# A transformer block's first stage: the modulation products moved from VectorE to TensorE, 256 output channels at a time, and the first weight chunk's products of half the tokens with channels outermost

## The chip, the cores and the metric

The kernel runs as one program on one core of a Trainium2 chip. The metric is the device time of one execution in microseconds (us), taken as the median of three runs. The profile shows one execution, with the engines TensorE (PE; its weight loads are listed apart as PEld), VectorE (DVE), ScalarE (ACT), GpSimd (POOL) and the queue engine SyncE (SP), which only issues transfers here.

## The reference

One layer of a hybrid block: a modulation of the normalised input, one combined input projection, attention and a state-space branch side by side, their merge, and a feed-forward part. All inputs are float32; there are 1024 tokens of 1024 channels. Only the opening matters here:

```python
mod = jax.nn.silu(c) @ w_ada[l] + b_ada[l]          # c: 1024, w_ada: 1024 x 6144
shift1, scale1, gate1, shift2, scale2, gate2 = [m[:, None, :] for m in jnp.split(mod, 6, axis=-1)]
h = rms_norm(x, norm1_w[l]) * (1.0 + scale1) + shift1
proj = h @ w_in[l]
q, k, v, xBC, z, dt_raw, gates = jnp.split(proj, offsets, axis=-1)
```

So the first projection can start on a channel block of `h` as soon as 128 channels of `scale1` and `shift1` are there, and each of these 128 values is a sum over all 1024 rows of `w_ada`.

## The kernel before, in words

**The products.** Every large product is done in three passes of a reduced-precision float type: an operand is split into a high part and a low remainder (`hi`, `lo`), and TensorE adds hi·hi, hi·lo and lo·hi. The activation `h` is kept transposed, channels on the partitions, as `hhi[k][half]` and `hlo[k][half]` (printed as `hh` and `hl`): eight blocks `k` of 128 channels, two halves of 512 tokens. A weight chunk comes as `traw` (256 of the 1024 input channels, 400 output columns), and is split into `twh` on ACT and `twl` on POOL or DVE. Four such chunks make the first group of columns, `g=0`; `gemm_tm` multiplies it with eight token tiles `t`, 96 products (3 passes x 8 channel blocks x 4 token tiles) for each half of the tokens, into banks called `psq`.

**The first stage (lines 257 to 362).** Two of the six slices of `w_ada` are wanted first, 4 MB each. `mod_acc` loads a slice in eight row blocks of 128 x 1024 (`wada`, rows of 4 KB) and sums them on DVE, weighted by silu(c), into `macc` (line 219 once, line 221 seven times). `mod_col` then adds up the partitions with products against a column of ones (line 227: eight products, one moving column each) and DVE adds the bias. `scale_col` makes `s1`, the scale with the norm weight. In the meantime the first four token tiles `xs` are loaded, squared and summed on ACT (line 282), scaled (line 292), transposed on TensorE (line 298, `pst`) and copied to `xT`. When scale and shift of all 1024 channels are there, ACT writes `hh` (line 305), DVE the same in full precision (line 309) and DVE or POOL the remainder `hl` (line 154, the line of a helper). Then come the 96 products of the first half, then the 32 transposes of the second half's tokens, its `hh` and `hl`, and its 96 products.

**What sets the order.** SP and DVE keep the order in which this stage is written (`manual_schedule`); the other engines' order is set by a scheduler, and what the scheduler puts into SP's or DVE's row from later code can stand between. Each engine works its row off in order, so whoever stands behind a waiting instruction waits too.

Of the kernel before, what the change touches and what calls it, by code (L numbers as in the profile page):

```python
# [9 lines left out]
F32 = mybir.dt.float32  # L10
# [8 lines left out]
P = 128  # L19
# [71 lines left out]
def block(ctx: ExitStack, tc: tile.TileContext, ia, out, upto=99, dbg=None):  # L91
# [61 lines left out]
    def tt(e, o, a, b, op):  # L153
        e.tensor_tensor(out=o, in0=a, in1=b, op=op)  # L154
# [75 lines left out]
    def scale_col(dst, mi, n0):  # L230
        V.scalar_tensor_tensor(out=dst, in0=modc[:, mi], scalar=1.0, in1=vecT[:, n0:n0 + 8], op0=ALU.add, op1=ALU.mult)
# [24 lines left out]
    psq = psqs.enter_context(tc.tile_pool(name="psq", bufs=1, space=PSUM, side="right", reuse_waits="tile"))  # L256
    with tc.tile_pool(name="p0", bufs=1) as p0, tc.tile_pool(name="ps0", bufs=1, space=PSUM) as ps0:
        rows = p0.tile([120, P], F32, name="rows1")
        rows2 = p0.tile([104, P], F32, name="rows2")
        crow = p0.tile([8, P], F32, name="crow")  # L260
        dma(crow, ia["c"][0].rearrange("(t p) -> t p", p=P))
        ps = ps0.tile([P, 512], F32, name="psv", tag="psv", bufs=2)
        T.transpose(ps[:, :8], crow, ident[:8, :8])
        A.activation(sc, ps[:, :8], AF.Silu)

        def load_rows():
            for r0, nm in ((BA, "b_ada"), (N1, "norm1_w"), (CB0, "conv_b"), (N2, "norm2_w"), (SN, "ssd_norm_w")):
                src = ia[nm][0].rearrange("(t p) -> t p", p=P)
                dma(rows2[r0:r0 + src.shape[0], :], src)
            ps = ps0.tile([P, 512], F32, name="psv", tag="psv", bufs=2)  # L270
            T.transpose(ps[:, :104], rows2, ident[:104, :104])
            V.tensor_copy(vecT, ps[:, :104])

        xs, xT = {}, {}
        ss = p0.tile([P, 8], F32, name="ss")
        rs = p0.tile([P, 8], F32, name="rs")

        def x_load(t):
            xs[t] = p0.tile([P, D], F32, name="xs", tag="xs", bufs=4)
            dma(xs[t], x_in[t * P:(t + 1) * P, :])  # L280
            junk = p0.tile([P, D], BF16, name="junk", tag="junk", bufs=1)
            A.activation(junk, xs[t], AF.Square, accum_out=ss[:, t:t + 1])

        def x_unit(half):

            h4 = slice(half * 4, half * 4 + 4)
            rstd(p0, rs[:, h4], ss[:, h4], D, 4, G)
            for t in range(half * 4, half * 4 + 4):
                if half and t % 2:
# [4 lines left out]
        def x_turn(half, k):  # L294

            ps = ps0.tile([P, 512], F32, name="pst", tag="pst", bufs=2)
            for t in range(4):
                T.transpose(ps[:, t * P:(t + 1) * P], xs[half * 4 + t][:, k * P:(k + 1) * P], ident)
            return ps

        def x_mod(half, turned):
            for k in range(KT):
                src = turned(k)
                hi, lo = hhi[k][half], hlo[k][half]
                A.activation(hi, src, AF.Identity, scale=s1[:, k:k + 1], bias=modc[:, 0, k:k + 1])  # L305
                if k % 2 == 0:
                    fb = p0.tile([P, D], F32, name="xf", tag="macc", bufs=2)
                f = fb[:, (k % 2) * 512:(k % 2 + 1) * 512]
                V.tensor_scalar(out=f, in0=src, scalar1=s1[:, k:k + 1], scalar2=modc[:, 0, k:k + 1], op0=ALU.mult, op1=ALU.add)
                late.append((G if k % 4 in LOG else V, lo, f, hi.bitcast(F32), ALU.subtract))  # L310
                while len(late) > 1:
                    tt(*late.pop(0))
            tt(*late.pop(0))

        late = []

        def mod1(sl, between=None):
            g = mod_acc(p0, sl, bufs=7)
            n = 0
            try:  # L320
                while True:
                    next(g)
                    n += 1
                    if between:
                        between(n)
            except StopIteration as e:
                return e.value

        def mod2(acc, mi, sl):
            ps = ps0.tile([P, 512], F32, name="psv", tag="psv", bufs=2)  # L330
            mod_col(acc, sl, mi, ps)

        with tc.manual_schedule(engines={mybir.EngineType.SP, mybir.EngineType.DVE}):
            def first_half(n):
                if n <= 4:
                    x_load(n - 1)
                if n == 4:
                    x_unit(0)
                    for k in range(KT):
                        xT[k] = p0.tile([P, 512], F32, name="xT", tag="xT", bufs=8)  # L340
                        A.copy(xT[k], x_turn(0, k))
                if n == 6:
                    load_rows()

            scale = mod1(1, first_half)
            shift = mod1(0)
            mod2(scale, 1, 1)
            scale_col(s1, 1, N1)
            mod2(shift, 0, 0)
            loads = qkv_loads(0, G)  # L350
            first = [f() for f in loads[:2]]
            for t in range(4, 8):
                x_load(t)
            first += [f() for f in loads[2:]]
            x_mod(0, lambda k: xT[k])
            dma(masks[:, 1:5], ia["masks"][:, 1:5])
            dma(rows, ia["conv_w"][0].rearrange("k (t p) -> (k t) p", p=P))
            x_unit(1)
            x_mod(1, lambda k: x_turn(1, k))
# [4 lines left out]
        return dict(hhi=hhi, hlo=hlo, s1=s1)  # L364


    def gemm_tm(psp, tag, bufs, n, loads, evac, nxt_loads, first=None):

        w = first or [f() for f in loads]
        nxt = []  # L370
        for t in range(NT):
            if t >= 4 and nxt_loads:
                nxt.append(nxt_loads[t - 4]())
            half, sl = t // 4, slice((t % 4) * P, (t % 4 + 1) * P)
            ps = psp.tile([P, 512], F32, name=tag, tag=tag, bufs=bufs)
            o = ps[:, :n]
            for k in range(KT):
                hi, lo = w[k // 2]
                T.matmul(o, hhi[k][half][:, sl], hi[:, k % 2, :n], start=k == 0, stop=False)  # L379
                T.matmul(o, hhi[k][half][:, sl], lo[:, k % 2, :n], start=False, stop=False)  # L380
                T.matmul(o, hlo[k][half][:, sl], hi[:, k % 2, :n], start=False, stop=k == KT - 1)  # L381
                if k % 2:
                    yield 6 * n / 2400.0
            evac(t, o)
        return nxt
# [31 lines left out]
    with tc.tile_pool(name="p1", bufs=1, reuse_waits="tile") as p1, \  # L417
# [87 lines left out]
        for g in range(NKV):  # L505
            raws = {}

            def evac(t, ps):
                half = t // 4
                if t % 4 == 0:  # L510
                    raws[half] = p1.tile([P, 4, QKV_N], F32, name="qkvr", tag="qkvr", bufs=2)
                A.copy(raws[half][:, t % 4], ps)  # L512
# [4 lines left out]
            first = pump(gemm_tm(psq, "psq", 4, QKV_N, qkv_loads(g), evac,  # L517
                                 qkv_loads(g + 1) if g + 1 < NKV else z_loads(0), first))

        def dt_stream():  # L520

# [826 lines left out]
    with tc.tile_pool(name="p6", bufs=1, reuse_waits="tile") as p6:  # L1348
# [446 lines left out]
```

## Time and profile before

| | us |
|---|---|
| median of three runs (2547.34 to 2552.68) | 2547.74 |
| the profiled execution's own time | 2555.1 |
| its span | 2553.3 |
| TensorE busy / share of the span | 2422.2 / 95% |
| VectorE busy / share | 1779.8 / 70% |
| ScalarE busy / share | 1121.7 / 44% |
| GpSimd busy / share | 908.8 / 36% |
| TensorE busy in the first 37.0 us | 13.9 |
| start of the first half's products / of the second half's | 37.0 / 69.3 |

Over the span TensorE is the engine that is nearly always busy, so a microsecond of it saved or lost counts, if it isn't made good by a wait that gets shorter. The beginning is the exception: in the first 37 us it is idle for most of the time. The profiled execution is 7.4 us above the median of the runs.

### The profile page before, as it was taken

Reading aid. Unit: us, or ns where it says so; the run is one execution under the profiler, and the core shown is the slowest. Engines: PE = TensorE matmul, PEld = TensorE weight load, DVE = VectorE, ACT = ScalarE, POOL = GpSimd, SP = SyncE. Lnnn points to the kernel's source line nnn. Section 1 sums busy time; section 2 is a strip of 40 time slices with the busy share of each in tenths; the row PEclk is TensorE's granted clock in tenths of the full one; section 3 lists DMA queues with packets and bytes.
Section 4 is the critical chain, followed back from the end, with each engine's and each line's share of the span. In section 5 each row is a group of like instructions: output and inputs, shape, how many; then the busy total and the mean of one; then the engine's idle time right before and its main releaser. Section 6 shows DMA issues by size and latency. Waiting matters only on the chain. (4 is left out here: it accounts for less than half of the span.)

```text
span 2553.3 us, 32339 instructions
## 1 busy us (share of the span) xinstructions
PE 2422.2 (95%) x11403; PEld 1935.0 (76%) x11403; DVE 1779.8 (70%) x2199; ACT 1121.7 (44%) x1944; POOL 908.8 (36%) x672
## 2 busy tenths in 40 slices
PE   5999999999989999999899999999898999999999
PEld 5898777777767777777667767777686888888887
DVE  5756346898866666666577787636659888667794
ACT  5455513444546666666333344343333222264430
POOL 2310107677711111110346665514107875113200
PEclk9899999999999999999999999999998999999999
DMA  7653751233541212111666675466424645464522
GB/s 262 181 164 124 231 182 62 78 96 92 165 141 58 87 54 88 55 54 50 201 194 206 190 218 164 146 197 207 152 79 140 201 151 171 177 207 132 161 84 89
DMA packets 282162, 363.38 MB, mean 142 GB/s; under 512 B 33673, under 2 KB 166513, under 8 KB 282001
## 3 DMA queue, kind: packets, MB, share of 16 engines
q1 hardware_dynamic: 209841, 285.22, 35.7%
q10 hardware_dynamic: 72160, 76.11, 8.9%
q8 instruction: 90, 1.47, 0.2%
q14 instruction: 71, 0.58, 0.1%
HBM read 248.18 MB, written 113.06 MB: 141 GB/s over the span
## 5 line engine op out<-in xcount | busy, mean ns | idle before, releaser
L891 DVE TENSOR_REDUCE nm<-pss 128x1 f32<-128x1024 f32 x128 | 156.7, 1225 | 135.1 <-PE pss L889 133.7
L380 PE MATMUL psq<-twl,hh 128*128 128x400 f32 (+1 forms) x512 | 193.1, 379 | 7.4 <-DVE twl L154 5.4
L379 PE MATMUL psq<-twh,hh 128*128 128x400 f32 (+1 forms) x512 | 192.4, 381 | 3.4 <-ACT hh L305 1.3
L381 PE MATMUL psq<-twh,hl 128*128 128x400 f32 (+1 forms) x512 | 191.7, 376 | 0.0
L893 ACT ACTIVATE pf<-pss,nm 128x1024 f32<-128x1024 f32 x128 | 142.8, 1116 | 102.1 <-PE pst L904 99.3
L154 DVE TENSOR_TENSOR pl<-pst,ph 128x512 fp32r<-128x512 f32 x256 | 167.9, 683 | 27.6 <-ACT ph L168 27.6
L904 PEld LDWEIGHTS pst<-masks,pf 128*128 128x128 f32 x1024 | 118.3, 140 | 70.1 <-issue 29.7
L168 ACT CAST ph<-pst 128x512 fp32r<-128x512 f32 x256 | 146.4, 585 | 54.2 <-PE pst L904 41.0
L904 PE MATMUL pst<-masks,pf 128*128 128x128 f32 x1024 | 157.0, 276 | 11.7 <-DVE pl L154 9.7
L713 DVE SCALAR_TENSOR_TENSOR cacc<-pad,cwT,cacc 128x1024 f32<-128x1024 f32 x96 | 163.2, 1730 | 0.4
L154 POOL TENSOR_TENSOR av<-av,rz 64x512 f32<-64x512 f32 x32 | 41.3, 1290 | 326.5 <-DMA rz<-rz 158.5
L1673 PE MATMUL p<-o,o 128*128 128x512 f32 x400 | 155.2, 389 | 0.6 <-DVE o L154 0.6
L1672 PE MATMUL p<-o,o 128*128 128x512 f32 x400 | 153.8, 390 | 1.7 <-DVE ac L154 1.4
L1674 PE MATMUL p<-o,o 128*128 128x512 f32 x400 | 153.8, 389 | 0.0
L168 ACT CAST wop<-ws 128x512 fp32r<-128x512 f32 x116 | 71.7, 621 | 103.6 <-PE pp L1332 67.5
L380 PEld LDWEIGHTS psq<-twl,hh 128*128 128x128 f32 x512 | 98.5, 192 | 19.6 <-DVE twl L154 6.5
L154 POOL TENSOR_TENSOR sl<-sl 128x512 f32<-128x512 f32 x32 | 49.6, 1553 | 178.5 <-DVE o L154 72.4
L379 PEld LDWEIGHTS psq<-twh,hh 128*128 128x128 f32 x512 | 97.8, 192 | 15.8 <-ACT qkvr L512 1.7
L381 PEld LDWEIGHTS psq<-twh,hl 128*128 128x128 f32 x512 | 97.8, 191 | 11.9 <-issue 0.9
L1106 ACT ACTIVATE e<-psd 128x512 f32<-128x512 f32 x128 | 70.8, 595 | 74.6 <-PE psd L1104 61.4
L168 ACT CAST o<-sl 128x512 fp32r<-128x512 f32 x92 | 56.9, 623 | 105.0 <-PE p L1674 88.4
L941 PE MATMUL pv<-pl,v 128*64 128x512 f32 x256 | 102.0, 419 | 0.0
(424 smaller groups left out, 7133.0 us busy)
## 6 DMA issues: line engine op xcount, KB each, us to landing
ar<-r SPq DMA_DIRECT2D x100, 256.0 KB
wada<-in_w_ada_dram SPq DMA_DIRECT2D x48, 512.0 KB
r<-in_w_mlp_dram SPq DMA_DIRECT2D x32, 512.0 KB
sl<-in_w_mlp_dram SPq DMA_DIRECT2D x64, 256.0 KB
r<-in_w_in_dram SPq DMA_DIRECT2D x26, 512.0 KB
r<-ro ACTq DMA_DIRECT2D x52, 256.0 KB
r<-as SPq DMA_DIRECT2D x48, 256.0 KB
xb<-cst ACTq DMA_DIRECT2D x20, 512.0 KB
```

The costliest lines, as they stand in the source:

```text
L154: e.tensor_tensor(out=o, in0=a, in1=b, op=op)
L168: (e_hi or A.copy)(hi, src)
L379: T.matmul(o, hhi[k][half][:, sl], hi[:, k % 2, :n], start=k == 0, stop=False)
L380: T.matmul(o, hhi[k][half][:, sl], lo[:, k % 2, :n], start=False, stop=False)
L381: T.matmul(o, hlo[k][half][:, sl], hi[:, k % 2, :n], start=False, stop=k == KT - 1)
L713: V.scalar_tensor_tensor(out=acc, in0=pad[:, k:k + S], scalar=cwT[:, 24 * k + i:24 * k + i + 1], in1=acc, op0=ALU.mult, op1=ALU.add)
L891: V.tensor_reduce(out=nm, in_=ps, axis=AX.X, op=ALU.max, negate=True)
L893: A.activation(pfs[u], ps, AF.Exp, bias=nm, accum_out=zall[:, u:u + 1])
L904: T.transpose(pt[:, k], pf[:, (hf * 4 + k) * P:(hf * 4 + k + 1) * P], ident)
L1672: T.matmul(ps, a[:, 0, sl], b[0], start=start, stop=False)
L1673: T.matmul(ps, a[:, 0, sl], b[1], start=False, stop=False)
L1674: T.matmul(ps, a[:, 1, sl], b[0], start=False, stop=stop)
```

## The change

The sums over `w_ada`'s rows leave DVE. `ada_load(kh)` loads, for 256 output channels, all 1024 rows of both slices: two transfers of 1 MB with rows of 1 KB, four times. `ada_mod(k)` forms the 128 values of scale and of shift for channel block `k` on TensorE: 2 x 8 products with a 128 x 128 block of `w_ada` as the stationary operand and one column of silu(c) as the moving one. DVE adds bias and norm weight per block. `x_mod(0, k)` follows for that block straight from the transposes' bank (the copy `xT` is gone), then `first_gemm(k - 1)`, the twelve products of the block before with four token tiles whose banks stay open over all eight blocks; `gemm_tm` is given these banks as `made` and skips their products. The loads of `x` all have their own buffers now; small vectors are loaded from ACT's queue into tiles of their own; the scale of the norm is worked out on DVE in place of POOL; in the first half DVE takes over all the remainders `hl`.

```diff
+        for r0, nm in ((BA, "b_ada"), (N1, "norm1_w"), (CB0, "conv_b"), (N2, "norm2_w"), (SN, "ssd_norm_w")):
+            src = ia[nm][0].rearrange("(t p) -> t p", p=P)
+            vr = p0.tile([src.shape[0], P], F32, name=f"rows_{nm}")
+            adma(vr, src)
...
-            xs[t] = p0.tile([P, D], F32, name="xs", tag="xs", bufs=4)
+            xs[t] = p0.tile([P, D], F32, name="xs", tag="xs", bufs=8)
...
-            rstd(p0, rs[:, h4], ss[:, h4], D, 4, G)
+            rstd(p0, rs[:, h4], ss[:, h4], D, 4)
...
+            hi, lo = hhi[k][half], hlo[k][half]
+            A.activation(hi, ps, AF.Identity, scale=s1[:, k:k + 1], bias=modc[:, 0, k:k + 1])
+            f = p0.tile([P, 512], F32, name="xf", tag="xf", bufs=4)
+            V.tensor_scalar(out=f, in0=ps, scalar1=s1[:, k:k + 1], scalar2=modc[:, 0, k:k + 1], op0=ALU.mult, op1=ALU.add)
+            late.append((G if half and k % 4 in LOG else V, lo, f, hi.bitcast(F32), ALU.subtract))
...
+        def ada_load(kh):
+            ada[kh] = p0.tile([P, 2, KT, 2 * P], F32, name="wada", tag="wada", bufs=2)
+            for j in range(2):
+                dma(ada[kh][:, j], w_ada[:, j * D + 2 * kh * P:j * D + 2 * (kh + 1) * P].rearrange("(r p) c -> p r c", p=P))
+
+        def ada_mod(k):
+            w = ada[k // 2]
+            ps = ps0.tile([P, 512], F32, name="psv", tag="psv", bufs=2)
+            for j in range(2):
+                for r in range(KT):
+                    T.matmul(ps[:, j:j + 1], w[:, j, r, (k % 2) * P:(k % 2 + 1) * P], sc[:, r:r + 1], start=r == 0, stop=r == KT - 1)
+            tt(V, modc[:, 0:2, k], ps[:, 0:2], vecT[:, BA + k:BA + k + 9:8], ALU.add)
+            V.scalar_tensor_tensor(out=s1[:, k:k + 1], in0=modc[:, 1, k:k + 1], scalar=1.0, in1=vecT[:, N1 + k:N1 + k + 1],
+                                   op0=ALU.add, op1=ALU.mult)
+
+        def first_gemm(k):
+            hi, lo = w0[k // 2]
+            for t in range(4):
+                o, sl = first_ps[t][:, :QKV_N], slice(t * P, (t + 1) * P)
+                T.matmul(o, hhi[k][0][:, sl], hi[:, k % 2, :QKV_N], start=k == 0, stop=False)
+                T.matmul(o, hhi[k][0][:, sl], lo[:, k % 2, :QKV_N], start=False, stop=False)
+                T.matmul(o, hlo[k][0][:, sl], hi[:, k % 2, :QKV_N], start=False, stop=k == KT - 1)
...
-            scale = mod1(1, first_half)
-            shift = mod1(0)
-            mod2(scale, 1, 1)
-            scale_col(s1, 1, N1)
-            mod2(shift, 0, 0)
...
+            for t in range(4):
+                x_load(t)
+            ada_load(0)
+            w0.append(loads[0]())
+            vectors()
+            x_unit(0)
+            w0.append(loads[1]())
+            ada_load(1)
             for k in range(KT):
+                if k == 2:
+                    for t in range(4, 8):
+                        x_load(t)
+                if k in (2, 4):
+                    w0.append(loads[k // 2 + 1]())
+                    ada_load(k // 2 + 1)
+                ada_mod(k)
+                x_mod(0, k)
+                if k:
+                    first_gemm(k - 1)
+                if k == KT - 2:
+                    x_unit(1)
             tt(*late.pop(0))
+            first_gemm(KT - 1)
...
-            for k in range(KT):
+            for k in range(KT if t >= len(made) else 0):
```

What the change does to the engines' rows stands at three places.

**TensorE at the start.** The row of before, from its first instruction to the first products of `g=0` (`macc` is DVE's sum, `psq` the product's bank):

```order
L263 MATMUL psv<-masks,crow 128x8
L271 MATMUL psv<-masks,rows_392 128x104
L298 MATMUL pst<-masks,xs 128x128 x8
L227 MATMUL psv<-ones,macc 128x1 x8
L298 MATMUL pst<-masks,xs 128x128 x24
L227 MATMUL psv<-ones,macc 128x1 x8
L379 MATMUL psq<-twh,hh_0_347 128x400
L380 MATMUL psq<-twl,hh_0_347 128x400
```

The row now, one turn of the loop later (`hh_0_349` is channel block 1, `hh_0_351` block 2; lines 331 to 333 are `first_gemm`, line 322 is `ada_mod`, of which all sixteen products of a block stand between the products of the block two before it):

```order
L331 MATMUL psq<-twh,hh_0_349 128x400
L332 MATMUL psq<-twl,hh_0_349 128x400
L322 MATMUL psv<-sc,wada 128x1 x11
L333 MATMUL psq<-twh,hl_0_365 128x400 x4
L322 MATMUL psv<-sc,wada 128x1 x5
L302 MATMUL pst<-masks,xs 128x128 x4
L331 MATMUL psq<-twh,hh_0_351 128x400
L332 MATMUL psq<-twl,hh_0_351 128x400
```

Instead of sixteen one-column products ahead of all others there are 128, of which 32 stand ahead of the first large product and 96 in runs between the large ones.

**ScalarE ahead of the third channel block.** Before, from the splits of the weight chunks on:

```order
L168 CAST twh<-traw 128x2x400 x2
L305 ACTIVATE hh_0_347<-xT,modc,s_331 128x512
L305 ACTIVATE hh_0_349<-xT,modc,s_331 128x512
L282 ACTIVATE junk,ss<-xs 128x1024
L305 ACTIVATE hh_0_351<-xT,modc,s_331 128x512
```

And now:

```order
L168 CAST twh<-traw 128x2x400 x2
L304 ACTIVATE hh_0_347<-pst,modc,s_331 128x512
L286 ACTIVATE junk,ss<-xs 128x1024 x2
L304 ACTIVATE hh_0_349<-pst,modc,s_331 128x512
L286 ACTIVATE junk,ss<-xs 128x1024 x2
L168 CAST twh<-traw 128x2x400 x2
L304 ACTIVATE hh_0_351<-pst,modc,s_331 128x512
```

The `hh` of block 2 now stands behind the squares of the second half's four token tiles and behind the splits of the third and the fourth weight chunk.

**SyncE's queue.** Before, the 16 row blocks of `w_ada` come first (the first four token tiles between them), then two weight chunks of four transfers each, then the second half of `x`. Now, from the second quarter of `w_ada` on:

```order
L315 DMA wada<-in_w_ada_dram 128x8x256 x2
L284 DMA xs<-in_x_dram 128x1024 x4
L244 DMA traw<-in_w_in_dram 128x2x256
L244 DMA traw<-in_w_in_dram 128x2x64 x2
L244 DMA traw<-in_w_in_dram 128x2x16
L315 DMA wada<-in_w_ada_dram 128x8x256 x2
L244 DMA traw<-in_w_in_dram 128x2x256
```

Ahead of these rows stand the first four token tiles, the first quarter of `w_ada` and two weight chunks. The fourth weight chunk (the last row) comes behind the third quarter of `w_ada`; the last quarter stands behind three chunks of the next group of columns.

More of the change, by code (lines that the diff above doesn't have):

```diff
@@ L264, in block, with vectors @@
         A.activation(sc, ps[:, :8], AF.Silu)
[L266 to L269, printed above, removed]
+        def vectors():
             ps = ps0.tile([P, 512], F32, name="psv", tag="psv", bufs=2)
-            T.transpose(ps[:, :104], rows2, ident[:104, :104])
+            for r0, vr in vrows:
+                n = vr.shape[0]
+                T.transpose(ps[:, r0:r0 + n], vr, ident[:n, :n])
             V.tensor_copy(vecT, ps[:, :104])
-        xs, xT = {}, {}
+        xs, ada, w0 = {}, {}, []
         ss = p0.tile([P, 8], F32, name="ss")
@@ L286, in x_unit @@
             h4 = slice(half * 4, half * 4 + 4)
-            rstd(p0, rs[:, h4], ss[:, h4], D, 4, G)
+            rstd(p0, rs[:, h4], ss[:, h4], D, 4)
             for t in range(half * 4, half * 4 + 4):
-                if half and t % 2:
+                if t % 2:
                     V.tensor_scalar(out=xs[t], in0=xs[t], scalar1=rs[:, t:t + 1], scalar2=None, op0=ALU.mult)
@@ L292, in x_unit, with x_mod @@
                     A.activation(xs[t], xs[t], AF.Copy, scale=rs[:, t:t + 1])
-        def x_turn(half, k):
+        def x_mod(half, k):
             ps = ps0.tile([P, 512], F32, name="pst", tag="pst", bufs=2)
@@ L298, in x_turn @@
                 T.transpose(ps[:, t * P:(t + 1) * P], xs[half * 4 + t][:, k * P:(k + 1) * P], ident)
-            return ps
-        def x_mod(half, turned):
-            for k in range(KT):
[L303 to L312, printed above, removed]
-            tt(*late.pop(0))
@@ L315, in block @@
[L315 to L338, printed above, removed]
-                    for k in range(KT):
[L340 to L343, printed above, removed]
-            scale = mod1(1, first_half)
-            shift = mod1(0)
-            mod2(scale, 1, 1)
-            scale_col(s1, 1, N1)
-            mod2(shift, 0, 0)
[L350 to L355, printed above, removed]
+            hi, lo = hhi[k][half], hlo[k][half]
@@ new lines, in x_mod @@
+            A.activation(hi, ps, AF.Identity, scale=s1[:, k:k + 1], bias=modc[:, 0, k:k + 1])
+            f = p0.tile([P, 512], F32, name="xf", tag="xf", bufs=4)
+            V.tensor_scalar(out=f, in0=ps, scalar1=s1[:, k:k + 1], scalar2=modc[:, 0, k:k + 1], op0=ALU.mult, op1=ALU.add)
+            late.append((G if half and k % 4 in LOG else V, lo, f, hi.bitcast(F32), ALU.subtract))
+            while len(late) > 1:
+                tt(*late.pop(0))
+        def ada_load(kh):
+            ada[kh] = p0.tile([P, 2, KT, 2 * P], F32, name="wada", tag="wada", bufs=2)
+            for j in range(2):
+                dma(ada[kh][:, j], w_ada[:, j * D + 2 * kh * P:j * D + 2 * (kh + 1) * P].rearrange("(r p) c -> p r c", p=P))
@@ new lines, in first_gemm @@
+        def first_gemm(k):
[5 more added lines that the diff above has]
+                T.matmul(o, hlo[k][0][:, sl], hi[:, k % 2, :QKV_N], start=False, stop=k == KT - 1)
+        late = []
+        first_ps = [psq.tile([P, 512], F32, name="psq", tag="psq", bufs=4) for t in range(4)]
@@ new lines, in block @@
+        with tc.manual_schedule(engines={mybir.EngineType.SP, mybir.EngineType.DVE}):
+            loads = qkv_loads(0, G)
+            for t in range(4):
[6 more added lines that the diff above has]
+            ada_load(1)
+            for k in range(KT):
+                if k == 2:
[10 more added lines that the diff above has]
+                    x_unit(1)
+            tt(*late.pop(0))
+            first_gemm(KT - 1)
@@ L356, in block @@
             dma(masks[:, 1:5], ia["masks"][:, 1:5])
             dma(rows, ia["conv_w"][0].rearrange("k (t p) -> (k t) p", p=P))
-            x_unit(1)
-            x_mod(1, lambda k: x_turn(1, k))
+            for k in range(KT):
+                x_mod(1, k)
+            tt(*late.pop(0))
+            first = w0
         ps = ps0.tile([P, 512], F32, name="psv", tag="psv", bufs=2)
@@ L364, in block, with gemm_tm @@
         return dict(hhi=hhi, hlo=hlo, s1=s1)
-    def gemm_tm(psp, tag, bufs, n, loads, evac, nxt_loads, first=None):
+    def gemm_tm(psp, tag, bufs, n, loads, evac, nxt_loads, first=None, made=()):
         w = first or [f() for f in loads]
@@ L374, in gemm_tm @@
             half, sl = t // 4, slice((t % 4) * P, (t % 4 + 1) * P)
-            ps = psp.tile([P, 512], F32, name=tag, tag=tag, bufs=bufs)
+            ps = made[t] if t < len(made) else psp.tile([P, 512], F32, name=tag, tag=tag, bufs=bufs)
             o = ps[:, :n]
-            for k in range(KT):
+            for k in range(KT if t >= len(made) else 0):
                 hi, lo = w[k // 2]
@@ L517, in block @@
             first = pump(gemm_tm(psq, "psq", 4, QKV_N, qkv_loads(g), evac,
-                                 qkv_loads(g + 1) if g + 1 < NKV else z_loads(0), first))
+                                 qkv_loads(g + 1) if g + 1 < NKV else z_loads(0), first, () if g else first_ps))
         def dt_stream():
```

3 lines of the change are left out of this document (2 added, 1 removed).

## The prediction

> **What bounds the kernel now.** I read the page first, then the first 100 us in order of time, then the stage in stretches, and last the granted clock in stretches of 3.41 us.
>
> ```profile
> PE 2422.2 (95%) x11403; PEld 1935.0 (76%) x11403; DVE 1779.8 (70%) x2199; ACT 1121.7 (44%) x1944; POOL 908.8 (36%) x672
> 0.00:37.00 37.00, 13.94 (x66) 0.99 0.93 335
> 37.00:58.50 21.50, 19.41 (x98) 0.93 0.55 154
> 58.50:69.20 10.70, 6.23 (x33) 0.75 0.62 217
> 37.03 0.70 PE L379 MATMUL psq<-twh,hh 128*128 128x400 f32 x1 [1.26 <-ACT hh L305]
> 69.32 0.70 PE L379 MATMUL psq<-twh,hh 128*128 128x400 f32 x1 [1.25 <-ACT qkvr L512]
> ```
>
> The first row is the page's. The next three are stretches of the first stage: length, TensorE's busy time and instructions, granted clock, the transfers' busy share, GB/s. TensorE carries the kernel (95%), but until 37 us it works 13.9 us, while the transfers are 93% busy: the stage waits for 8 MB of `w_ada`. Then the first half's 96 products take to 58.5, and the second half's transposes and remainders to 69.32, where the second half's products begin. Behind that point the two programs have nearly the same order on all engines, with TensorE busy nearly throughout, so I take what is gained or lost at this point as gained or lost at the end. The question is when TensorE gets there.
>
> **The prices.** Rows of the order of time: start, duration, engine, line, count.
>
> ```profile
> 24.22 3.54 PEld L227 LDWEIGHTS psv<-ones,macc 128*128 128x128 f32 x16
> 33.83 1.86 PEld L227 LDWEIGHTS psv<-ones,macc 128*128 128x128 f32 x16 [0.99 <-DVE macc L221]
> 258.57 1.86 PEld L227 LDWEIGHTS psm<-ones,macc 128*128 128x128 f32 x16
> 27.70 5.50 PE L298 MATMUL pst<-masks,xs 128*128 128x128 f32 x24
> 58.49 1.03 PE L298 MATMUL pst<-masks,xs 128*128 128x128 f32 x8
> 38.53 0.54 PE L379 MATMUL psq<-twh,hh 128*128 128x400 f32 x1
> 38.86 0.54 PE L380 MATMUL psq<-twl,hh 128*128 128x400 f32 x1
> 40.47 0.34 PE L381 MATMUL psq<-twh,hl 128*128 128x400 f32 x1
> 40.65 0.34 PE L379 MATMUL psq<-twh,hh 128*128 128x400 f32 x1
> ```
>
> A one-column product with a 128 x 128 float32 block shows as two passes (8 products, 16 rows); a pass costs its weight load, 1.86/16 = 0.116 us, or 3.54/16 = 0.22 us at half clock. A transpose takes 0.13 or 0.23 us, a 400-column product (start to start) 0.18 or 0.33 us. The new `ada_mod` is of the same shape as line 227: 128 products, 256 passes, 29.7 us at the full clock and 56.6 at half. Removed are 32 passes (3.54 + 1.86 = 5.4 us, in time that was idle anyway), sixteen sums on DVE and eight copies on ACT; these lay ahead of 37 us beside the transfers, and give nothing but the earlier start. The vector loads on ACT's queue (five small ones ahead of `sc`) and the rest of `x_unit` are over before the first quarter of `w_ada` lands; I take them at nothing, and at 1 to 2 us of a later start if they were not.
>
> **When TensorE can start.**
>
> ```profile
> 5.65 0.75 DVE L219 TENSOR_SCALAR macc<-wada,sc 128x1024 f32<-128x1024 f32 x1 [4.65 <-DMA wada<-in_w_ada_dram]
> 14.74 1.06 ACT L282 ACTIVATE junk<-xs 128x1024 bf16<-128x1024 f32 x1 [1.41 <-DMA xs<-in_x_dram]
> 1934.00:1939.00 5.00, 4.38 (x19) 1.00 1.05 359
> 40.00:44.00 4.00, 4.00 (x24) 1.00 1.09 273
> ```
>
> Between the first and the eighth 512 KB transfer lie 9.09 us, 1.30 us each. Now four tiles of `x` come first: 5.65 to 9.6. The two halves of the first quarter have rows of 1 KB; a stretch in which the MLP's weights come with such rows moved 359 GB/s, so 2.9 us for 1 MB: 12.5 and 15.4. That is 24.5 us ahead of today's first product. TensorE then has 64 passes and eight transposes ahead of the first large product (channel blocks 0 and 1): at half clock 64 x 0.22 + 8 x 0.23 = 15.9 us, so 28.4.
>
> **Which clock.** Stretches of 3.41 us, cut where the granted clock changes; the fourth number is the clock. It is shown as 1.00 up to the first recorded change at 36.3, but the durations above tell that up to about 33 it was half.
>
> ```profile
> 26.11:29.52 3.41, 3.41 (x18) 1.00 1.03 417
> 29.52:32.94 3.42, 3.42 (x17) 1.00 1.11 329
> 32.94:36.35 3.41, 2.20 (x18) 1.00 0.88 266
> 36.35:39.76 3.41, 2.73 (x8) 0.51 1.01 391
> 46.59:50.00 3.41, 1.67 (x10) 1.00 0.00 0
> 60.24:63.66 3.42, 1.57 (x10) 1.00 0.56 212
> 63.66:67.07 3.41, 2.63 (x13) 0.51 0.99 370
> ```
>
> The clock changes at the ends of such stretches, by what TensorE did in them. 2.73 us of large products lifted it, 2.63 us of transposes did not: about 78% of a stretch. 1.67 us of large products kept it, 1.57 us of transposes did not: about 48%. Two rows tell of one-column products. The first is full (1.6 us of line 227, the rest transposes), yet the transposes behind it still ran at 0.23; the second stretch, full of transposes alone, lifted the clock. And 32.94 to 36.35 held 2.20 us, far over 48%, nearly all of it line 227, and the clock fell. So one-column products count for little or nothing. The Trainium skill, "TensorE: Matmul & The Clock Gate", "What's actually happening", gives the same window of 3413 ns and just the two clocks. Its section "HAM oscillation — how this bites in real kernels" draws the rule that TensorE stays fast as long as it has no idle gap over 3.4 us; by that the change would keep the full clock and end up near +9 us (the first rival below), not +35. The trace does not agree as far as one-column products fill the time: the clock fell after a stretch without any idle gap over 1 us.
>
> Now the loop: per channel block 32 passes, 4 transposes, 12 products. At full clock 3.7 + 0.5 + 2.2 = 6.4 us, at half 7.1 + 0.9 + 4.0 = 12.0 us. What counts is (0.5 + 2.2)/6.4 = 42% or 4.9/12.0 = 41%: too little to keep the clock. It is lifted only when a stretch falls almost wholly into the transposes and eight products that stand together (0.9 + 2.7 = 3.6 us at half clock). 78% of a stretch is 2.66 us, so of its 3.41 us of possible places 3.6 + 3.41 - 2 x 2.66 = 1.7 us do, one in two; the next stretch then does 6.8 us of work in 3.4. So 12.0 - 1.7 = 10.3 us a block.
>
> **The sum.** 28.4, then six blocks with `ada_mod` in them, 61.8: 90.2. The last 24 products and eight transposes hold no one-column products, 9.8 us at half clock; the clock rises after one stretch, 6.6 us: 96.8. Then the remaining 24 transposes, paced by ACT and DVE through two banks: before, 32 took from 58.5 to 69.32, 1.35 us for four; six times that is 8.1: the second half's products start at 104.9, against 69.32, +35.6. Both times the clock is then low or about to fall, which I take as equal (it cost 2.3 us before, bounds -2.3 to +2.3). One wait behind this point gets shorter:
>
> ```profile
> 97.14 0.46 PE L380 MATMUL psq<-twl,hh 128*128 128x400 f32 x1 [3.64 <-DVE twl L154]
> ```
>
> TensorE waits there for a remainder of the second group; now 27 products of the second group stand ahead of it, not 23, so 4 x 0.18 = 0.7 us less. In all +34.9, say +35: 2590 us against the profiled execution's 2555.1. That lies 7.4 us above the median of the runs, so 2583 by the median.
>
> The queues, edit by edit.
>
> ```profile
> 34.02 0.86 ACT L168 CAST twh<-traw 128x800 fp32r<-128x800 f32 x1 [0.20 <-DMA traw<-in_w_in_dram]
> 36.17 1.52 ACT L305 ACTIVATE hh<-xT,modc,s 128x512 fp32r<-128x512 f32 x2
> 39.08 0.68 DVE L154 TENSOR_TENSOR hl<-xf,hh 128x512 fp32r<-128x512 f32 x1
> ```
>
> ACT's `hh` of block 2 now stands behind the split of the fourth weight chunk, whose transfer stands behind the third quarter of `w_ada`: from 15.4, two chunks (0.82 MB at the 273 GB/s of 40 to 44 us, in which two such chunks came; 3.0), 5.8, four tiles 5.2, a chunk 1.5, 5.8, a chunk 1.5 are 38.2, then 0.86 for the split and 0.76 for `hh`: 39.8. At half clock TensorE comes to that product at 28.4 + 2 x 12 = 52, so this wait costs nothing; at full clock it does (below). The last quarter of `w_ada` waits behind three chunks of the next group; these wait for splits of about 42, so it lands near 52, and is wanted at half clock near 80, at full clock near 56. The remainders moved from POOL to DVE (0.68 us each) and the norm's scale lie beside 12 us of TensorE per block. The second half's `x` has its own buffers and is scaled in block 6, which takes that wait (ahead of 58 us before) off the path; it is already in the 8.1.
>
> **The rivals.**
> - One-column products count as work and the clock stays full from its first lift. Ahead of the first large product stand 8.5 us of full-clock work, some 5 us of it at half: 12.5 + 11 = 23.5. Two turns of 6.4 later, at 36.3, TensorE waits for the `hh` of block 2 to 39.8; from there six times 2.2, four `ada_mod` (14.8) and six groups of transposes (3.1, two of them the second half's): 70.9, with 8.1 more 79.0, +9.7 - 0.7 = +9: 2557. For it speaks only that busy time as the profile counts it would be nearly 100%; against it the two rows above.
> - The same without that wait (the scheduler's order on ACT costs nothing because transfers are faster): 3.5 us less, +5.5: 2553.
> - The clock stays at half through the whole loop: 28.4 + 6 x 12.0 + 9.8 + 8.1 = 118.3, +48: 2596. It would take stretches that never fall into the 3.6 us; the place of these stretches against the program is not mine to know.
> - Faster: the weight loads of the one-column products hide beside the large products. From 39.8 only 13.2 + 3.1 and 128 passes would be left; with those at nothing the second half starts at 64.2, -5.1 - 0.7 = -5.8: 2542. The point from which it decides is 5.8 us over 128 passes, 0.045 us each. Against it: 0.116 us each where sixteen stand in a row, also at 258.57 between large products, and here they stand in runs of 10 to 22.
> - The change doesn't do what it says: excluded by the order of the rows, where the products have moved.
>
> **How the numbers follow.** Mixed clock 66%, full clock with the wait 15%, without it 5%, half throughout 8%, hidden loads 4%, others (a start later by microseconds, another wait) 2%. The likeliest gives 2583; its own range, by the place of the stretches and by whether a one-column product counts for nothing or for a third, is 2572 to 2594. The range reaches down to the full clock with its wait and up to the half clock: 2556 to 2596, which leaves out about 1 in 10. About 5 us (0.2%) is what a measurement of this kernel can tell from no change: faster 4%, same 5% (half of the full clock without a wait, and some of the others), slower 91%.
>
> **What would show it.** Right: in the stage's stretches TensorE is busy from about 12.5 us on, the granted clock is 0.5 in most stretches between 36 and 90 us, passes of line 322 take 0.22 us, the first large product starts near 28, the second half's first (line 387) near 105, and behind it all is as before, 35 us later. Wrong: passes of 0.116 us throughout with line 387 starting at 75 to 82 (one-column products count); a wait of TensorE for line 304 near 40 us would go with it; or a stretch of DVE or of transfers as releaser of line 322, which would mean that a queue I took at nothing holds it.

## The result and the profile after

| | before | after |
|---|---|---|
| median of the runs (4 each) | 2548.84 us (2547.34 to 2552.68) | 2581.27 us (2575.21 to 2583.35) |
| ratio, 95% interval | | 1.0121 [1.0100, 1.0142] |
| the profiled execution; its span | 2555.1; 2553.3 us | 2579.94; 2578.1 us |
| TensorE busy | 2422.2 us (95%) | 2474.8 us (96%) |
| second half's first product | 69.32 us | 103.94 us |

The change makes the kernel 32.4 us slower by the medians (25 to 36 by the interval). TensorE is the engine that carries the kernel, and it has more to do: the page's row after, and the groups of the first 125 us that belong to the new products.

```profile
PE 2474.8 (96%) x11631; PEld 1990.4 (77%) x11631; DVE 1768.8 (69%) x2212; ACT 1116.6 (43%) x1934; POOL 901.7 (35%) x658
```

```profile
L322 PE MATMUL psv<-sc,wada 128*128 128x1 f32 x256 | 47.5, 316 | 5.5 <-DMA wada<-in_w_ada_dram 5.5
L331 PE MATMUL psq<-twh,hh 128*128 128x400 f32 x32 | 17.4, 544 | 0.0
```

The 256 one-column passes keep TensorE busy for 47.5 us. At the full clock they would take 29.7 (256 x 0.116). The large products suffer too: 544 ns each, where a product at full clock shows 340. Now the same stage in order of time (start, duration, engine, line, count):

```profile
13.24 4.82 PE L322 MATMUL psv<-sc,wada 128*128 128x1 f32 x22 [5.55 <-DMA wada<-in_w_ada_dram]
...
19.12 8.53 PE L322 MATMUL psv<-sc,wada 128*128 128x1 f32 x40
...
28.26 0.68 PE L331 MATMUL psq<-twh,hh 128*128 128x400 f32 x1
...
31.08 2.38 PE L322 MATMUL psv<-sc,wada 128*128 128x1 f32 x20
...
36.80 0.68 PE L331 MATMUL psq<-twh,hh 128*128 128x400 f32 x1
...
39.62 4.69 PE L322 MATMUL psv<-sc,wada 128*128 128x1 f32 x22
...
48.74 0.68 PE L331 MATMUL psq<-twh,hh 128*128 128x400 f32 x1
...
57.28 0.68 PE L331 MATMUL psq<-twh,hh 128*128 128x400 f32 x1
...
60.09 3.83 PE L322 MATMUL psv<-sc,wada 128*128 128x1 f32 x18
...
68.85 0.68 PE L331 MATMUL psq<-twh,hh 128*128 128x400 f32 x1
...
77.39 0.68 PE L331 MATMUL psq<-twh,hh 128*128 128x400 f32 x1
...
88.96 0.68 PE L331 MATMUL psq<-twh,hh 128*128 128x400 f32 x1
...
96.15 1.04 PE L302 MATMUL pst<-masks,xs 128*128 128x128 f32 x8
...
103.94 0.70 PE L387 MATMUL psq<-twh,hh 128*128 128x400 f32 x1 [1.25 <-ACT qkvr L520]
```

The reader sees TensorE start at 13.24 and a pass take 8.53/40 = 0.21 us, and less in a few stretches, as at 31 (2.38/20 = 0.12). The loop's last passes end near 88; then come the last products, the second half's transposes, and at 103.94 the product that stood at 69.32 before. The stage in stretches of 4 us (length, TensorE's busy time and count, granted clock, share of the transfers, GB/s):

```profile
36.00:40.00 4.00, 4.00 (x16) 0.50 1.14 297
...
52.00:56.00 4.00, 4.00 (x32) 0.90 1.09 354
56.00:60.00 4.00, 4.00 (x16) 0.50 0.19 60
60.00:64.00 4.00, 4.00 (x20) 0.50 0.00 0
...
72.00:76.00 4.00, 4.00 (x32) 0.93 0.00 0
...
88.00:92.00 4.00, 4.00 (x16) 0.50 0.00 0
```

TensorE has no gap in any of these rows, and yet the clock is at half in most of them. From 60 us on no transfer runs either, so nothing but TensorE holds the stage.

### The profile page after: what moved, and what is told of

It is laid out like the page before. It is cut to its first block, busy times and chain, and to the rows that moved or that the text cites. A ratio compares the mean times of both kernels' runs of the same rounds, so it can differ in the third digit from the quotient of the medians.

```text
span 2578.1 us, 32744 instructions
## 1 busy us (share of the span) xinstructions
PE 2474.8 (96%) x11631; PEld 1990.4 (77%) x11631; DVE 1768.8 (69%) x2212; ACT 1116.6 (43%) x1934; POOL 901.7 (35%) x658
## 5 line engine op out<-in xcount | busy, mean ns | idle before, releaser
L387 PE MATMUL psq<-twh,hh 128*128 128x512 f32 (+1 forms) x480 | 179.7, 379 | 2.1 <-ACT qkvr L520 1.2
L388 PE MATMUL psq<-twl,hh 128*128 128x512 f32 (+1 forms) x480 | 180.1, 376 | 1.0 <-DVE twl L154 1.0
L389 PE MATMUL psq<-twh,hl 128*128 128x512 f32 (+1 forms) x480 | 180.4, 377 | 0.0
L387 PEld LDWEIGHTS psq<-twh,hh 128*128 128x128 f32 x480 | 90.9, 190 | 14.5 <-ACT twh L168 1.6
L388 PEld LDWEIGHTS psq<-twl,hh 128*128 128x128 f32 x480 | 91.1, 190 | 12.2 <-DVE twl L154 1.8
L389 PEld LDWEIGHTS psq<-twh,hl 128*128 128x128 f32 x480 | 91.1, 190 | 11.6 <-issue 0.9
```

## The experiments

The theory: a one-column product costs its weight load and counts for almost nothing in what the clock is granted by. So the loop runs mostly at half clock (24 of the 34 us at the second half's start) and holds 256 passes that were not there (10 us). Rivals: the passes cost only because they stand between the large products; the reordered products cost by themselves; the loads or another queue hold the loop. All ratios are to the kernel before, run beside the experiment; in brackets the 95% interval. The column "start" is the second half's first product in the profile.

| | what | start, us | ratio |
|---|---|---|---|
| E0 | before, again | 69.9 | one run, 2554.71 us |
| E1 | 64 columns | 79.8 | 1.0014 [1.0004, 1.0023] |
| E2 | one of eight row blocks | 68.9 | 0.9986 [0.9977, 0.9995] |
| E3 | sums on VectorE | 83.4 | 1.0045 [1.0030, 1.0060] |
| E4 | 16 columns | 103.0 | 1.0085 [1.0067, 1.0102] |
| E5 | first part alone | 98.0 | 1.0071 [1.0057, 1.0085] |
| E6 | second part alone | 71.7 | 1.0000 [0.9989, 1.0010] |
| E7 | shared sums | 82.9 | 1.0021 [1.0013, 1.0030] |
| E8 | E7, sums sooner | 74.6 | 0.9996 [0.9986, 1.0006] |
| E9 | after, again | 104.5 | 1.0117 [1.0098, 1.0136] |
| E10 | E8, blocks in pairs | 69.9 | 0.9987 [0.9977, 0.9996] |
| E11 | 32 columns | 81.5 | 1.0037 [1.0022, 1.0052] |

**E0, the kernel before, unchanged.** No edit.

> The kernel before, unchanged, for a second profile of it. Open is where 10 us went: in the two profiles shown, the changed kernel is 34.6 us late at the first product of the second half, 24.5 us late at 725 us and at the end, while the medians differ by 32.4. Theory A: the profile of before was of an execution that lost some 6 us between 100 and 725 us for reasons of its own. Then this profile's own time is near the median, 2548, and its attention stage (line 889) begins near 718, not at 724.4. Theory B: the changed program makes good 10 us there in every execution, since waits behind the first stage get shorter. Then line 889 begins at 724 again.

The first product of the attention's line 889 (897 after) starts at 722.4 us here, against 724.7 in the first profile of before and 749.2 after: between the 718 of theory A and the 724 of theory B. This execution's own time, 2554.71, is again above the median of the runs beside it (2553.06). So 2.3 us of what the first pair of profiles shows as made good behind the stage belong to the profiled execution of before itself; the larger part does not.

**E1, 64 moving columns.**

```
-  T.matmul(ps[:, j:j + 1], w[...], sc[:, r:r + 1], ...)
+  T.matmul(ps[:, j * 64:(j + 1) * 64], w[...], sc[:, r:r + 1].to_broadcast([P, 64]), ...)
-  tt(V, modc[:, 0:2, k], ps[:, 0:2], ...)
+  tt(V, modc[:, 0:2, k], ps[:, 0:128:64], ...)
```

> The changed kernel with 64 equal moving columns in place of one in each of the 128 modulation products; results and weight loads are the same. Theory (one-column products don't count for the clock): 64 columns fill more than half of a pass, so the stage's stretches hold well over 48% of counted work, the clock stays at 1.0 from its first lift on, a pass takes 0.12 us, ScalarE's hh of block 2 becomes a wait of some 3 to 6 us near 40 us, and the second half's first product starts near 79 instead of 104: about 2557 us. Rival (passes are dear by their number and the clock does not depend on the columns, only on weight loads or on idle time): the clock stays at 0.5 in most stretches, passes take 0.22 us or more, the start is at 104 or later: 2581 us or more.

The products are the same in number and place, each now writes 64 equal columns. A row of the order of time and one of the stretches:

```profile
37.01 3.46 PE L322 MATMUL psv<-sc,wada 128*128 128x64 f32 x30
```

```profile
60.00:64.00 4.00, 4.00 (x33) 1.00 0.01 4
```

A pass takes 3.46/30 = 0.115 us with 64 columns as with one at the full clock, and the stretch that was busy 4.00 us at clock 0.50 after is busy 4.00 us at clock 1.00 here. The second half starts at 79.8, 24 us sooner, and nine tenths of the loss are gone. So the clock is what costs, and it does not follow the busy time; whether it follows the columns moved or a least width of a product is for E4 and E11. The wait of TensorE for `hh` of block 2 did not come: the scheduler had put that `hh` ahead of the split of the fourth weight chunk, and it ran at 36.55.

**E2, one of the eight row blocks in each sum.** `for r in range(KT)` in `ada_mod` becomes one step, so this kernel leaves out seven eighths of each sum.

> The changed kernel with one of the eight row blocks in each modulation sum: 16 products in place of 128; seven eighths of the sum over the rows of the modulation matrix are left out. All transfers stay. Theory (the passes and the clock that they cost are the whole loss): the stage is then held by ScalarE's hh of block 2 near 41 and by the last quarter of the modulation matrix near 54 us, the second half starts at 66 to 69 as before the change, and the time is 2544 to 2549. Rival (the new order of the queues, ScalarE's splits and squares ahead of hh, costs as much by itself): the second half starts later than 75 and the time stays over 2556.

With 224 of the passes gone the start is at 68.9 and the time 0.9986: without the passes the loss is gone. It is also about as early as this order starts the second half: the loads run up to 48 us (332 GB/s on average from 12 on), then come, among others, these two rows of the order of time.

```profile
52.83 1.70 PE L332 MATMUL psq<-twh,hl 128*128 128x400 f32 x4 [3.66 <-DVE hl L154]
...
68.91 0.70 PE L386 MATMUL psq<-twh,hh 128*128 128x400 f32 x1 [1.25 <-ACT qkvr L519]
```

**E3, the sums on VectorE**, eight operations of 128 x 2 x 256 per quarter, and one product with ones for each column. The remainders still due are written ahead of each sum.

```
+  V.tensor_scalar(out=acc, in0=ada[kh][:, :, 0], scalar1=sc[:, 0:1], ...)
+  V.scalar_tensor_tensor(out=acc, in0=ada[kh][:, :, r], scalar=sc[:, r:r + 1], in1=acc, ...)   # r = 1 to 7
-  for r in range(KT): T.matmul(ps[:, j:j + 1], w[...], sc[:, r:r + 1], ...)
+  T.matmul(ps[:, j:j + 1], acc[...], ones[:, 0:1], start=True, stop=True)
```

> The changed kernel with the sums over rows back on VectorE, 256 channels of scale and shift at a time (eight operations of 512 elements for each quarter, in place), and 16 one-column products against ones. So only the second part of the change, channels outermost and loads by 256 channels, is done. Theory: the loss lies in the one-column products; VectorE needs some 10 us per quarter (5.3 of sums, 4 of what it does for two blocks), from 15.5 on, so the last block is there near 56, the second half starts at 64 to 68, and the time is 2541 to 2549, at or below that before. Rival (channels outermost costs by itself, by open banks or by its order): over 2556.

The start came later than expected, at 83.4. VectorE's rows, and GpSimd's of the same time:

```profile
16.48 8.47 DVE L327 SCALAR_TENSOR_TENSOR wada<-wada,sc 128x512 f32<-128x512 f32 x7
...
31.75 6.98 DVE L327 SCALAR_TENSOR_TENSOR wada<-wada,sc 128x512 f32<-128x512 f32 x7
...
46.82 5.47 DVE L327 SCALAR_TENSOR_TENSOR wada<-wada,sc 128x512 f32<-128x512 f32 x7
```

```profile
18.69 4.15 POOL L154 TENSOR_TENSOR twl<-traw,twh 128x800 fp32r<-128x800 f32 x2 [18.25 <-ACT twh L168]
34.69 1.92 POOL L154 TENSOR_TENSOR twl<-traw,twh 128x800 fp32r<-128x800 f32 x1 [11.85 <-ACT twh L168]
```

Each quarter's sums, `s`, `xf` and `hl` stand one behind the other on VectorE, and TensorE waits for them (8.2 us the first time). VectorE is the bound in its turn: better than the change, worse than before. The time, 2564.4, lies where the rival had it (over 2556), but not for the rival's reason: E6 below shows that channels outermost costs nothing by itself.

**E4 and E11, 16 and 32 columns**: E1's edit with 16 and 32 in place of 64.

> The changed kernel with 16 equal moving columns in each modulation product instead of one (E1 had 64): a smaller dose of the same thing. Theory A (the clock is granted by moving columns, not by busy time): 16 columns fill 16/128 of the time in which a pass occupies TensorE, so a block's counted share rises from about 0.42 to 0.42 + 0.58 x 0.12 = 0.49. That is at the edge of what kept the full clock in the stretches of before (0.48) and far from what lifted it (0.78), so most of the loop stays at half clock: the second half's first product at 90 to 104, the time 1.006 to 1.012 of before. Theory B (any product wider than one column counts as full work): full clock from about 31 as in E1, the second half at 80, the time 1.000 to 1.003 of before.

> The changed kernel with 32 equal moving columns in each modulation product: between E4 (16, which stayed at half clock) and E1 (64, full clock). By the rows, 400 columns take 0.18 us, so 32 take 0.014 of a pass's 0.116 us, 12%; E1's 64 take 25% and E4's 16 take 6%. Theory A (columns are counted, and about 48% of a stretch keeps the clock): counted shares at full clock 0.42 + 0.58 x 0.12 = 0.49 here, 0.56 for E1, 0.46 for E4; at the edge, so the clock falls now and then: the second half's first product at 80 to 98, the time 1.002 to 1.009. Theory B (a threshold on the product's width itself, between 16 and 64): all or nothing, either as E1 (80, 1.001) with the clock full throughout or as E4 (103, 1.0085).

One stretch of E4, three of E11:

```profile
72.00:76.00 4.00, 4.00 (x19) 0.50 0.00 0
```

```profile
60.00:64.00 4.00, 4.00 (x34) 1.00 0.01 4
64.00:68.00 4.00, 4.00 (x24) 0.68 0.00 0
68.00:72.00 4.00, 4.00 (x25) 0.89 0.00 0
```

With 16 columns the loop is mostly at half clock from 46 us on and the start is at 103.0; with 32 the clock holds to 64, falls for one stretch (0.68 and 0.89 over 4 us each are 3.4 us at half clock), and the start is at 81.5; with 64 it does not fall in the loop. So the effect grows with the dose. A column takes 0.18/400 us, so 16, 32 and 64 columns fill 6, 12 and 25% of a pass of 0.116 us, and a block's counted shares at full clock are 0.46, 0.49 and 0.56: below, at and above the 48% that the prediction read from the stretches of before. (The expectations of E1 and E4 took more for a column: over half of a pass for 64, an eighth for 16.) E11 fits theory A: neither all of E1 nor E4. The 48% itself rests on two stretches of before and on these doses, and is no closer known than that.

**E5, the first part alone.** `first_gemm` and `first_ps` are taken out, so the 96 products stand behind the loop in the old order.

> The first part of the change alone: the modulation matrix by 256 channels and its sums on TensorE, but the first weight chunk's products in the old order, token tile by token tile, behind the loop. Theory A (the loss is the 256 passes at half clock, whatever stands between them): 13.2 + 256 passes x 0.22 = 56 + 32 transposes x 0.23 = 7 gives about 76 with the loads of x and weights under it, less some 4 for the passes that still run at full clock; then the 96 large products, the first ones at half clock (0.33 each for 4 to 7 us), the others at 0.18: 20 more, and 8 for the transposes of the second half: its first product at 97 to 106, the time 1.008 to 1.014 of before, as the whole change. Theory B (the passes cost because they stand between the large products and break their clock): without the mixture the second half starts at 90 or sooner and the time is 1.006 or less.

```profile
66.08 6.83 PE L322 MATMUL psv<-sc,wada 128*128 128x1 f32 x32
...
77.71 0.34 PE L384 MATMUL psq<-twl,hh 128*128 128x400 f32 x1
```

The loss is there without the mixture, 1.0071, though a little less than expected (1.008 to 1.014). All passes take 6.83/32 = 0.213 us up to 73.7, but the large products, together now, lift the clock after 4 us and nearly all run at 0.18 us instead of 0.33.

**E6, the second part alone**, on the kernel before: `first_gemm(k - 1)` behind block k of `x_mod(0, ...)`.

> The second part of the change alone: the kernel before, modulation by whole rows on VectorE and GpSimd, but the first weight chunk's products of the first four token tiles with channels outermost, each block behind the next one's ScalarE and VectorE work. Theory A (this part is worth nothing by itself: before, TensorE waited only 2.1 us for a weight half and 1.3 us for an hh tile inside these products): the second half's first product at 67 to 71, the time 0.998 to 1.001 of before. Theory B (the reordering costs by itself, since the four sums are now all finished at the end and their evictions come in one bunch): the second half's first product at 72 or later, or the bunch's wait moved behind it, the time 1.002 or more.

```profile
PE psq L393 <- DVE twl L154: 4.2, 1, 4.2
```

By itself the order of the products changes nothing: 1.0000. The start is 1.8 us later than in E0, and the wait for a remainder behind it (4.2 us here, 2.7 and 3.6 in the two profiles of before) is still there.

**E9, the changed kernel again**, beside another set of runs of before.

> The changed kernel as it is, a second time, beside the same runs of the kernel before as E8. It is to tell how much of its loss the second part of the change (channels outermost) makes with the first, since E5 without it took 1.0071 [1.0057, 1.0085]. Theory A (mixing the large products into the passes makes them run at half clock: 44 of the 96 products or so at 0.33 instead of 0.18 us, 6 us): 1.010 to 1.013 again, the second half's first product at 101 to 106. Theory B (the 1.012 of the first measurement lay high by the chip or the runs): 1.006 to 1.009, as E5.

1.0117 again, as theory A had it: the second part, worth nothing alone, costs about 0.5% (1.0117 against 1.0071, the intervals apart) when the passes are there, since it puts the large products among them. In the profiles the start moves from 98.0 to 104.5, which is 6.5 us, while 0.46% are 12. Another 3 us of these are lost in the 185 us behind the start: E5 begins there at full clock (0.45 us for the first product), the changed kernel at half (0.70). The rest stays open.

**E7, E8 and E10, a version built from these.** 64 columns; rows 0 to 3 of each quarter summed on VectorE in place, 4 to 7 on TensorE, with a product by ones for VectorE's part; the second half's transposes inside the loop.

```
...
+  if k % 2 == 0: ada_sum(k // 2)          # E7; E8 and E10: quarters 2 and 3 behind x_mod(0, 3) and x_mod(0, 5)
   ada_mod(k)                              # E10: ada_mod(k) and ada_mod(k + 1) at even k
   x_mod(0, k)
   if k: first_gemm(k - 1)
-  if k == KT - 2: x_unit(1)
+  if k == 3: x_unit(1)
+  if k > 3: x_mod(1, 2 * (k - 4)); x_mod(1, 2 * (k - 4) + 1)
...
-  for k in range(KT): x_mod(1, k)         # behind the loop
```

> A candidate, built from what E1 to E3 showed: 64 columns (the clock stays full), four of the eight row blocks of each quarter summed on VectorE in place and the other four on TensorE with one product by ones for VectorE's part (160 passes instead of 256, 11 us less of TensorE), and the transposes of the second half inside the loop from the fourth channel block on instead of behind it. Theory A (TensorE is the bound of E1's loop, VectorE of E3's, so half each takes both below the loads, which end at 48): last quarter at 48, two blocks of 160/8 x 2 = 40 passes x 0.115 = 4.6, 24 products x 0.18 = 4.3 and 8 transposes = 1, some waits of 4: the second half's first product at 60 to 68, the time 0.994 to 0.999 of before. Theory B (VectorE's chain of sums, s, xf and hl in one queue is the bound as in E3, and the second half's transposes now wait in it too): second half at 72 to 82, the time 1.000 to 1.005.

```profile
45.93 0.43 PE L328 MATMUL psv<-ones,wada 128*128 128x64 f32 x2 [2.84 <-DVE wada L321]
...
66.04 0.69 PE L328 MATMUL psv<-ones,wada 128*128 128x64 f32 x2 [3.71 <-DVE wada L321]
```

The time, 1.0021, is in theory B's range, and the start, 82.9, just behind it (72 to 82): TensorE waits for sums that stand on VectorE behind work nobody waits for yet, and runs at half clock after each of the two waits.

> E7 with VectorE's sums of the third and fourth quarter put earlier in VectorE's queue: directly behind the xf of the first half's blocks 3 and 5, ahead of the second half's scaling and of the second half's xf, where E7 had them behind. Theory A (E7 lost 2.8 and 3.7 us of TensorE waiting for these sums, and with each wait a stretch at half clock, 44 to 56 and 64 to 76 us): without the waits the clock stays full; passes 160 x 0.116 = 18.6, 16 groups of transposes 8.5, 96 products 17.3, 4 more for the half clock at the start, from 13.2 on: 61.6, with some waits 62 to 70 for the second half's first product, the time 0.995 to 0.999 of before. Theory B (what stands behind TensorE's start is bound by the loads, which end at 48, and by ScalarE and VectorE in turn, so that waits only move): 74 to 82, the time 1.000 to 1.003.

The waits for these sums fell from 7.1 us to 1.4, and the time is that of before. Theory A had the start too early (62 to 70, here 74.6, in theory B's range); the time lies between the two. One row of VectorE shows what was left: the `s` of block 7 comes only here.

```profile
67.76 1.03 DVE L330 SCALAR_TENSOR_TENSOR s<-modc,vecT 128x1 f32<-128x1 f32 x1
```

> E8 with the modulation products of both channel blocks of a quarter together, ahead of the first of the two blocks' transposes and hh, so that the odd block's modulation does not stand on VectorE behind the second half's xf (in E8 block 7's sums were through TensorE at 61.4, but s for it came at 67.8). Theory A (the tail of E8 is this order on VectorE): block 7's hh 4 to 6 us sooner, the second half's first product at 67 to 72, the time 0.997 to 0.9995 of before. Theory B (the remaining distance is swallowed behind this point, as E6's and E1's late starts were, or the wait moves to hl): 72 to 76 or an unchanged time, 0.999 to 1.001.

```profile
69.91 0.45 PE L399 MATMUL psq<-twh,hh 128*128 128x400 f32 x1
```

The start is at 69.9, as before, and at the full clock (0.45, where before shows 0.70 after its wait). 0.9987 [0.9977, 0.9996] is some 3 us, as theory A had it. It is only just told from no gain, and this is the one version here with all its sums that comes out ahead of before.

## Why the prediction was right

The forecast was 2583 us, +35; measured 2581.27 and +32.4, and again 2582.36 and +30.5 in E9. The mechanism, passes at half clock in a loop that is lifted now and then, is what the runs show. Its terms by their own steps:

| term | forecast | measured |
|---|---|---|
| TensorE's start | 12.5 | 13.24 |
| 64 passes and 8 transposes at half clock | 15.9 | 15.0 (13.24 to 28.26) |
| six blocks at a mixed clock | 61.8 | 60.7 (28.26 to 88.96) |
| last 24 products and 8 transposes | 6.6 | 7.2 (88.96 to 96.15) |
| 24 transposes of the second half | 8.1 | 7.8 (96.15 to 103.94) |
| start of the second half | 104.9 | 103.94 |

The blocks show the mixed clock itself. Between the rows of line 331 at 28.26, 36.80, 48.74, 57.28, 68.85, 77.39 and 88.96 lie 8.54 us three times and 11.57 to 11.94 three times, where the prediction had 12.0 and, one time in two, 3.4 less; in E9's profile three blocks are again short and three long.

**The clock.** The step that decided, that one-column products count for little or nothing, is shown by E1, E11 and E4, in that order of dose. The rule of the Trainium skill weighed in the prediction ("TensorE: Matmul & The Clock Gate", "HAM oscillation — how this bites in real kernels": fast as long as there is no idle gap over 3.4 us) is not borne out: from 56 to 64 us TensorE was busy 8.00 of 8.00 us at clock 0.50. The first rival, full clock, is the kernel of E1. That its start, 79.8, lies near the 79.0 of that rival is luck: the first large product came at 28.68 and not at 23.5, and the wait for `hh` up to 39.8, which the 79.0 contains, did not come. Its price by the ratio is 3.6 us (1 to 6) and not 9.

**The queues** were rightly taken at nothing. `hh` of block 2 was ready at 41.85 + 0.77 = 42.6, wanted at 48.74; forecast 39.8 and 52.

```profile
41.85 0.77 ACT L304 ACTIVATE hh<-pst,modc,s 128x512 fp32r<-128x512 f32 x1
```

The last quarter was asked for only at 48.2, when TensorE's passes over the second quarter had ended and its buffer was free, a wait that the prediction's working does not have. It cost nothing: the transfers of the stage ended by 60, and the quarter was wanted at 71.66.

**The term that was mis-sized** is what lies behind the point: the prediction gave it -0.7, "TensorE waits there for a remainder", and took the rest as equal. Two stretches, E0's and after's first 30 us behind the second half's start:

```profile
69.90:100.00 30.10, 27.33 (x132) 0.90 0.54 157
```

```profile
103.90:134.00 30.10, 30.02 (x148) 0.90 0.57 163
```

In the same time TensorE gets through 148 instructions instead of 132, 16 x 0.18 = 2.9 us. The wait for `twl` is not 0.7 us shorter but gone (0.4 us of it are left in E9): VectorE had 34 us more for it. The clock in the two stretches, which the prediction took as equal, is equal: 0.90.

From the second half's start to line 570 (578 after) it is 187.9 us in E0 and 184.5 after (185.2 in E1); in E2, which starts as before does, it is 187.0, so the gain comes with the late start. Between there and the attention's product of line 889 another 4 to 5 us go (464.5 us in E0, 460.7 after, 459.5 in E9); TensorE's busy time over the same 1959 instructions falls by 2.8 and 5.5 us, so this is mostly clock (0.98 in E0, 0.99 after and in E9). Behind that product the distance stays: 26.8 us there and at line 1053 of before, 26.3 at line 1332, 25.2 at the end (after against E0).

To take what is lost at this point as lost at the end was therefore too much by 9 us in the profiled pair, and by 2 to 4 us by the medians, which lie 30 and 32 us apart. How much of the 4 to 5 us is chance of where the clock's stretches fall stays open; the same part takes 463.7 us in E1, 462.5 in E2 and 466.9 in E11, in no order of their starts. The two profiled executions, on which the working can be followed, lie 24.8 us apart (2579.94 against 2555.1), where it has 34.9: that the median comes within 2 us of the forecast is in part luck.

**The loss by parts**: +34.6 us at the second half's start. E1 leaves 10 of it at full clock, the bare passes; 24 are the clock. Of these 24, some 6 come from mixing the large products in (E5, 98.0 against 103.94).

## What to carry to other kernels

Read the granted clock and the columns together, not TensorE's busy time: a run of one-column products looks 100% busy and pulls its neighbours to half speed. If such products must stand among large ones, widen them with equal columns up to what their weight load hides (64 cost nothing here), or give half of the sum to another engine. Before moving sums from idle time under a transfer onto the engine that carries the kernel, count its passes at both clocks.

## What was not expected of the hardware

Widening a float32 product from one to 64 columns cost no time (0.115 us a pass, 0.116 with one). VectorE's 128 x 512 sums took 5.47/7 = 0.78 us alone, but in E3 the first seven took 3.0 us more while GpSimd subtracted for 4.15 us, the second seven 1.5 us more while it did so for 1.92: VectorE lost about three quarters of the time that GpSimd worked. The Trainium skill, "GPSIMD Engine Reference", "Key points", says that the two share their SBUF interfaces and contend when VectorE has two SBUF inputs, as these sums have; the rows agree, and give the price. E8 shows such a wait by itself: the `s` of block 7 above, 0.16 us in E3, took 1.03 and ended at 68.79, where by this profile GpSimd's subtraction ended (68.77).

```profile
67.13 1.64 POOL L154 TENSOR_TENSOR hl<-xf,hh 128x512 fp32r<-128x512 f32 x1 [4.86 <-DVE xf L306]
```

And the profile's clock can mislead until its first recorded change: in E5 it reads 1.00 for the stretch 60 to 64, while passes take 0.213 us, those of half clock.

```profile
60.00:64.00 4.00, 4.00 (x20) 1.00 0.00 0
```
